# GpSimd's arithmetic moved to VectorE in every layer, and the side tasks of the first feed forward layer left unsplit

## The chip, the cores and the metric

The kernel runs on one core of a Trainium2 chip. A core has TensorE (PE) for matmuls, VectorE (DVE), ScalarE (ACT) and GpSimd (POOL) for work on elements, and queues that start DMA transfers; almost all of these are started from SyncE (SP). The time is the device time of one execution in microseconds (us), the median of 3 runs, lower is better.

## The reference

The program is a net of two blocks over 256 tokens of width 1024, all in fp32:

```python
def first_block(x, ...):
    for l in range(2):
        h = rms_norm(x, norm_mix[l])
        x = x + hybrid_mixer(h, w_in[l], ...)
        h2 = rms_norm(x, norm_mlp[l])
        x = x + jnp.square(jax.nn.relu(h2 @ w_up[l])) @ w_down[l]     # 1024 -> 4096 -> 1024
...
def second_block(x, mem, ...):
    mem_n = rms_norm_2(mem, mem_norm_g)
    for i in range(2):
        u = rms_norm_2(h, mix_norm_g[i])
        # i = 0: hyena (short convolution, then two long ones by FFT with filters from a small sine net)
        # i = 1: attention with 12 query heads and 4 key heads
        main = ...
        cross = memory_cross_attn(cq, mem_n, w_mem_kv[i])
        h = h + jnp.concatenate([main, cross], axis=-1) @ w_out[i]
        h = h + expert_choice_ffn(rms_norm_2(h, ffn_norm_g[i]), ...)  # 16 experts, 32 tokens each
    return rms_norm_2(h, final_norm_g)
```

The hyena filters and the keys and values of the memory `mem` depend on no token: they can be made at any time before the hyena layer.

## The kernel before

The stages run one after the other: mixer 0, feed forward 0, mixer 1, feed forward 1 (block 1), then hyena, experts 0, attention, experts 1 (block 2). The residual `X` stays in SBUF, and weights stream in once, through a ring of buffers (`ring.one`, `load`, line 187).

**Split products.** A dense product in fp32 is done as three matmuls in the faster format fp32r (`mm3`, lines 303 to 306): high part by high part, and two cross terms. For the weights `split` (lines 284 to 293) makes the parts: ScalarE writes `hi` (line 291), and the subtraction for `lo` (line 292) goes to the next engine of a cycle, which each stage sets: `LO0` for both feed forward layers (`mlp`, line 964), `LO1` for the hyena layer (line 1310), `LO2` for attention (line 1438), `LO3` for the attention's output product (line 1562). The mixers have VectorE alone (line 822).

```python
    lo_engines = [cycle((V,))]
    LO0 = (G, V)
...
        S.activation(hi, src, AF.Copy)
        next(lo_engines[0]).tensor_tensor(lo, src, hi.bitcast(F32), op=ALU.subtract)
```

**Order of the work.** `Pipe` (lines 89 to 135) takes units, each with a `prep` (the splits) and a `run` (the matmuls), and prepares two units ahead of the one that runs. After each unit it steps the side tasks, generators that go on to their next `yield`. A scheduler then orders each engine's instructions when the program is built.

**Feed forward** (`mlp`, lines 963 to 1025): in eight rounds of 512 hidden columns, `up` gives ReLU (line 1007), square `r` (line 1008), its high part `hh` (line 1009) and low part `hlo` (line 1012); `down` adds into four accumulators `acc`.

**Side tasks of feed forward 0.** `filters_task` makes the hyena filters: two sine layers (`sin_layer`, lines 1046 to 1061), then four rounds (two filters, two halves of 384 channels). A round makes `hd` by split matmuls (lines 1122 and 1123), adds its absolute values into `sab` (line 1130, GpSimd), forms sum and difference `hx` and splits those into `hs` (line 1137, GpSimd), sums `sab` over the tokens (`psn`, line 1142) into `nrm`, and transforms by `mm3` with `fFh`, `fFl` into `kx`. `memory_task` (line 1161 on) normalises `mem` (`Norm`, transposes at line 344, `xl` at line 348) and makes keys and values of two layers from `nm.xh` and `nm.xl` with split weights.

**Hyena** (`hyena_layer`): four `chain` tasks carry the long convolutions beside the projections; GpSimd has `ya` (line 1375), four of the sixteen `yl` (line 1380) and three `al` (line 1401). **Attention**: GpSimd makes the rotated copies `rot` (line 1466). **Routing** of the experts (`id`, `sel`, `rp`, `affb`, lines 1573 to 1654) and the product with the last gain use GpSimd too.

Of the kernel before, what the change touches and what calls it, by code (L numbers as in the profile page):

```python
# [12 lines left out]
F32 = mybir.dt.float32  # L13
# [5 lines left out]
ALU = mybir.AluOpType  # L19
# [180 lines left out]
def build(ctx, tc, I, C, out, upto="all", dbg=None):  # L200
# [78 lines left out]
    LO0 = (G, V)  # L279
    LO1 = (G, V)  # L280
    LO2 = (V, G, V)
    LO3 = (G, V)
# [43 lines left out]
    class Norm:  # L326
# [706 lines left out]
    def stream(units, pool):  # L1033

        ahead = deque()
        for u in units + [None, None]:
            if u:
                hl.append(pool)
                u.prep()
                hl.pop()  # L1040
                ahead.append(u)
            if len(ahead) == 3 or not u:
                ahead.popleft().run()
            yield

# [17 lines left out]
    def filters_task(ring, kd):  # L1063

        with tc.tile_pool(name="fl", bufs=1) as fp:
# [26 lines left out]
            hst = fp.tile([128, T], F32R, name="fhst")  # L1092
# [3 lines left out]
            S.activation(hst, h2, AF.Copy)  # L1096
            V.tensor_tensor(hst[64:], h2[64:], hst[64:].bitcast(F32), op=ALU.subtract)
# [5 lines left out]
            for o in range(2):  # L1103
                for n in range(2):
                    c = slice(384 * n, 384 * n + 384)
                    w3 = fp.tile([128, 2, 384], F32, name="fw3")
                    for d in range(2):
                        nc.sync.dma_start(w3[64 * d:64 * d + 64], I["hy_filt_w3_2"][0].rearrange("k (o d c) -> k o d c", o=2, d=2)[:, o, :, c])
                    w3h = fp.tile([128, 2, 384], F32R, name="fw3h")
                    w3l = fp.tile([64, 2, 384], F32R, name="fw3l")  # L1110
                    S.activation(w3h, w3, AF.Copy)
                    G.tensor_tensor(w3l, w3[:64], w3h[:64].bitcast(F32), op=ALU.subtract)
                    hs = {op: [fp.tile([128, 2, 384], F32R, tag=f"h{op}{i}", name="hs") for i in range(2)] for op in (ALU.add, ALU.subtract)}
                    sab = fp.tile([128, 384], F32, tag="sab", name="sab")
                    yield
                    for t in range(2):
                        hd = []
                        for d in range(2):
                            h = fp.tile([128, 384], F32, tag=f"hd{d}", name="hd")
                            ps = A("psf", [128, 384])  # L1120
                            sl = slice(t * 128, (t + 1) * 128)
                            PE.matmul(ps, hst[:, sl], w3h[:, d], start=True, stop=False)
                            PE.matmul(ps, hst[:64, sl], w3l[:, d], start=False, stop=True)
                            V.tensor_tensor(h, ps, dec[:, t, c], op=ALU.mult)
                            if t == 0 and d == 0:
                                S.activation(sab, h, AF.Abs)
                            else:
                                ab = fp.tile([128, 384], F32, tag="ab", name="ab")
                                S.activation(ab, h, AF.Abs)
                                G.tensor_tensor(sab, sab, ab, op=ALU.add)  # L1130
                            hd.append(h)
                        yield
                        for op, dst in hs.items():
                            x = fp.tile([128, 384], F32, tag="hx", name="hx")
# [10 lines left out]
                    for part, op in ((0, ALU.add), (1, ALU.subtract)):  # L1145
# [3 lines left out]
                        for t in range(2):  # L1149
                            mm3(pp[t], Fh[:, t, part], Fl[:, t, part], hs[op][0][:, t], hs[op][1][:, t], True, True)  # L1150
# [10 lines left out]
    def memory_task(ring, mp, sp, m, kvd):  # L1161

        nm = Norm(m, gain("mem_norm_g_2"), mp, A)
        yield from nm.task(lambda n: True)
        for l in range(2):
# [3 lines left out]

            def put_k(j, ps):  # L1170
                V.tensor_tensor(kv[:, 0], ps, nm.R[:, None, :].to_broadcast([128, 2, T]), op=ALU.mult)

            def put_v(ps):
                for t in range(2):
                    evac(kv[:, 1, t], ps[t][:, :256], t, nm.r[:, t:t + 1])
# [133 lines left out]
    def hyena_layer(hy, ring, nm, c2, kd, kvd, state):  # L1309
# [29 lines left out]
        def chain(o, n):  # L1339
# [22 lines left out]
            for f in range(2):  # L1362
# [24 lines left out]
            for cb in range(3):  # L1387
# [9 lines left out]
                if o:  # L1397
# [3 lines left out]
                    (V if n else G).tensor_tensor(al[:, b], sz, ah[:, b].bitcast(F32), op=ALU.subtract)  # L1401
# [35 lines left out]
    def attention_layer(late, pool, ring, nm, c2, kvd, state, wqk):  # L1437
# [17 lines left out]
        def rotate(i):  # L1455
# [7 lines left out]
            for t in range(2):  # L1463
                for j, a, nh in ((1, 768, 4), (0, 512, 4)) if i else ((0, 0, 8),):
                    for g in range(2):
                        G.tensor_tensor(hx(rot[:, t, a:a + 64 * nh])[:, :, :, g], hx(qk[:, t, a:a + 64 * nh])[:, :, :, 1 - g],
# [367 lines left out]
    def mlp0_tasks(ring):  # L1834
        yield from filters_task(ring, kd)
        with tc.tile_pool(name="memp", bufs=1) as mp, tc.tile_pool(name="mems", bufs=3) as sp:
# [4 lines left out]
            yield from memory_task(ring, mp, sp, m, kvd)  # L1841
# [183 lines left out]
```

## Time and profile before

| what | value |
|---|---|
| median of 3 runs | 1873.15 us (1870.21 to 1873.5) |
| the profiled execution | 1872.64 us, span 1870.8 us |
| mean granted clock of TensorE | 0.959 of full speed |
| TensorE busy | 1628.8 us, 87% of the span |
| VectorE busy | 985.2 us, 53% |
| ScalarE busy | 676.6 us, 36% |
| GpSimd busy | 315.1 us, 17% |

The page comes from one execution. A share is the busy time over the whole span, so it mixes stages with different limits. "Idle before" is the time that an engine waited ahead of an instruction, with what ended the wait.

### The profile page before, as it was taken

How to read it: one execution, taken by the hardware profiler on the slowest of the kernel's cores; microseconds unless marked ns; L12 is line 12 of the kernel's file. 1: busy time of each engine (PE TensorE's matmuls, PEld its weight loads, DVE VectorE, ACT ScalarE, POOL GpSimd, SP SyncE). 2: the span in 40 equal slices, each digit the busy share in tenths (PEclk: the TensorE clock that was granted, in tenths of full speed). 3: DMA queues.
4: the chain of work that ended last, by engine and by line, in shares of the span. 5: the costliest groups of instructions: out<-in, count | busy, mean ns of one | idle time of the engine just before them, and what ended most of it. 6: DMA issues, size and time to landing. Idle time of an engine off the chain costs nothing. (4 is left out here: it accounts for less than half of the span.)

```text
span 1870.8 us, 27208 instructions
## 1 busy us (share of the span) xinstructions
PE 1628.8 (87%) x11139; PEld 1195.2 (64%) x11139; DVE 985.2 (53%) x1740; ACT 676.6 (36%) x1118; POOL 315.1 (17%) x216
## 2 busy tenths in 40 slices
PE   8999999998999999999989988666667989776765
PEld 7998977788999989999878844212224655221221
DVE  6998686775579977645578752000006862110102
ACT  6446454554454555544445331000003652000001
POOL 1000026654300000444333300000002210000001
PEclk9999999999999999999999988898989999899888
DMA  7543564454644436755244689999998759999997
GB/s 257 160 137 125 172 201 160 164 203 161 209 142 147 130 124 203 278 185 196 99 153 157 254 353 425 425 426 424 426 405 315 272 203 401 425 425 425 425 421 274
DMA packets 136516, 490.41 MB, mean 262 GB/s; under 512 B 11153, under 2 KB 32068, under 8 KB 115912
## 3 DMA queue, kind: packets, MB, share of 16 engines
q1 hardware_dynamic: 135919, 488.11, 69.2%
q8 instruction: 87, 1.43, 0.3%
q10 hardware_dynamic: 472, 0.57, 0.1%
q14 instruction: 38, 0.30, 0.0%
HBM read 483.41 MB, written 5.24 MB: 261 GB/s over the span
## 5 line engine op out<-in xcount | busy, mean ns | idle before, releaser
L291 ACT ACTIVATE hi<-w 128x1024 fp32r<-128x1024 f32 (+3 forms) x330 | 328.0, 997 | 323.7 <-PE psT L306 162.3
L304 PE MATMUL psT<-xh,hi 128*128 128x256 f32 x1328 | 386.8, 291 | 0.9 <-ACT hi L291 0.9
L305 PE MATMUL psT<-xh,lo 128*128 128x256 f32 x1328 | 378.6, 285 | 4.6 <-POOL lo L292 2.7
L306 PE MATMUL psT<-xl,hi 128*128 128x256 f32 x1328 | 378.7, 285 | 0.0
L292 DVE TENSOR_TENSOR lo<-w,hi 128x1024 fp32r<-128x1024 f32 (+3 forms) x245 | 285.3, 1165 | 141.5 <-ACT hi L291 140.6
L292 POOL TENSOR_TENSOR lo<-w,hi 128x1024 fp32r<-128x1024 f32 (+1 forms) x85 | 205.0, 2413 | 590.2 <-ACT hi L291 584.6
L305 PEld LDWEIGHTS psT<-xh,lo 128*128 128x128 f32 x1328 | 256.4, 193 | 9.5 <-POOL lo L292 3.3
L304 PEld LDWEIGHTS psT<-xh,hi 128*128 128x128 f32 x1328 | 256.5, 193 | 9.2 <-issue 6.4
L306 PEld LDWEIGHTS psT<-xl,hi 128*128 128x128 f32 x1328 | 256.1, 193 | 1.4 <-issue 1.1
L1741 PE MATMUL psx<-w,late 128*32 128x256 f32 (+1 forms) x1024 | 154.4, 549 | 75.8 <-DMA w<-in_exp_w_gate 39.5
L1741 PEld LDWEIGHTS psx<-w,late 128*32 128x32 f32 x1024 | 47.1, 116 | 180.5 <-issue 74.9
L1741 PE MATMUL psx<-w,xg 128*32 128x256 f32 (+1 forms) x1024 | 124.3, 547 | 35.2 <-DMA w<-in_exp_w_up 19.7
L1793 PE MATMUL psy<-w,late 128*32 128x512 f32 x576 | 98.8, 601 | 33.7 <-DMA w<-in_exp_w_down 29.8
L1777 ACT ACTIVATE yy<-psy,rslot 128x512 fp32r<-128x512 f32 (+1 forms) x17 | 11.3, 662 | 320.6 <-PE psy L1793 253.7
L1741 PEld LDWEIGHTS psx<-w,xg 128*32 128x32 f32 x1024 | 40.5, 117 | 115.7 <-issue 60.6
L306 PE MATMUL acc<-lo,hh 128*128 128x512 f32 x256 | 100.8, 394 | 3.0 <-POOL lo L292 3.0
L305 PE MATMUL acc<-hi,hlo 128*128 128x512 f32 x256 | 100.8, 394 | 0.0
L304 PE MATMUL acc<-hi,hh 128*128 128x512 f32 x256 | 100.5, 392 | 0.0
L1778 DVE SCALAR_TENSOR_TENSOR yy<-psy,rslot,yy 128x512 fp32r<-128x512 f32 (+1 forms) x17 | 12.2, 720 | 162.0 <-ACT yy L1777 161.5
L1757 DVE TENSOR_TENSOR late<-late,psx 128x512 f32<-128x512 f32 (+1 forms) x16 | 8.1, 550 | 166.3 <-PE psx L1741 166.3
L1793 PEld LDWEIGHTS psy<-w,late 128*32 128x32 f32 x576 | 27.1, 110 | 101.1 <-DMA w<-in_exp_w_down 49.8
L1756 DVE SCALAR_TENSOR_TENSOR late<-psx,rslot,late 128x512 f32<-128x512 f32 (+1 forms) x16 | 9.1, 613 | 152.3 <-ACT late L1755 152.3
(495 smaller groups left out, 2850.1 us busy)
## 6 DMA issues: line engine op xcount, KB each, us to landing
w<-in_exp_w_gate SPq DMA_DIRECT2D x64, 1536.0 KB, 27.6
w<-in_exp_w_up SPq DMA_DIRECT2D x64, 1536.0 KB, 29.5
w<-in_exp_w_down SPq DMA_DIRECT2D x48, 1536.0 KB, 26.9
w<-in_w_in SPq DMA_DIRECT2D x39, 1024.0 KB, 5.2
w<-in_w_up SPq DMA_DIRECT2D x32, 1024.0 KB, 5.6
w<-in_w_down SPq DMA_DIRECT2D x32, 1024.0 KB, 7.1
w<-in_exp_w_down SPq DMA_DIRECT2D x18, 1024.0 KB, 14.2
w<-in_w_out SPq DMA_DIRECT2D x10, 1024.0 KB, 5.6
```

The lines of the kernel that those rows point to most:

```text
L291: S.activation(hi, src, AF.Copy)
L292: next(lo_engines[0]).tensor_tensor(lo, src, hi.bitcast(F32), op=ALU.subtract)
L304: PE.matmul(ps, lh, rh, start=start, stop=False)
L305: PE.matmul(ps, ll, rh, start=False, stop=False)
L306: PE.matmul(ps, lh, rl, start=False, stop=stop)
L1741: mm = PE.matmul(pg[nm][n][32 * e:32 * e + 32, :c1 - c0], xg[gr // 2][:, k, 128 * (gr % 2) + 32 * e:128 * (gr % 2) + 32 * e + 32], wt[e][: ...
L1756: V.scalar_tensor_tensor(sg[:, :n], pg["gate"][i][:, :n], r2, sg[:, :n], op0=ALU.mult, op1=ALU.mult)
L1757: V.tensor_tensor(hid[:, c], sg[:, :n], pg["up"][i][:, :n], op=ALU.mult)
L1777: S.activation(yh, py, AF.Copy, scale=rs[:, 2, gr:gr + 1])
L1778: V.scalar_tensor_tensor(yl, py, rs[:, 2, gr:gr + 1], yh.bitcast(F32), op0=ALU.mult, op1=ALU.subtract)
L1793: PE.matmul(py[n][32 * e:32 * e + 32], hT[:, k, 32 * e:32 * e + 32], wt[e][:, k - k0, 512 * n:512 * n + 512], start=k == 0, stop=k == 5, t ...
```

## The change

VectorE takes the subtractions for `lo` everywhere, and the single operations of the hyena layer, of attention and of the filters that GpSimd had. In the side tasks of feed forward 0 the splits are gone: filters and memory products run as plain fp32 matmuls, the two halves of `hd` in the upper and the lower 64 rows of the array (`tile_position`). The filter's third weight is loaded as [128, 384], half as many bytes, and in two buffers. The ring load of `const_fwd` in the filters becomes one direct load of the quarter that is used. The pool `mems` and the function `stream` go, and the side tasks have 64 steps in place of 70. GpSimd keeps its memsets, the routing and the last product: 45 rows of the order in place of 122; VectorE has 1528 in place of 1445, ScalarE 720 in place of 757, TensorE 7320 in place of 7563, SP 175 in place of 176.

```diff
-    LO0 = (G, V)
-    LO1 = (G, V)
-    LO2 = (V, G, V)
-    LO3 = (G, V)
+    LO0 = (V,)
+    LO1 = LO2 = LO3 = (V,)
...
         def __init__(self, src, g, pool=None, psum=None, split=True):
-            if split:
+            self.x = None
+            if split is None:
+                self.x = pool.tile([128, 8, T], F32, name="xT")
+            elif split:
...
+                    if self.x is not None:
+                        S.activation(self.x[:, k], ps[:, j], AF.Copy, scale=self.g[:, k:k + 1])
+                        continue
...
     def filters_task(ring, kd):
-            raw = ring.one(C["fwd"]).rearrange("p t (s f) -> p t s f", s=2)[:, :, :, :128]
-            Fh = fp.tile([128, 2, 2, 128], F32R, name="fFh")
-            Fl = fp.tile([128, 2, 2, 128], F32R, name="fFl")
-            S.activation(Fh, raw, AF.Copy)
-            V.tensor_tensor(Fl, raw, Fh.bitcast(F32), op=ALU.subtract)
+            F = fp.tile([128, 2, 2, 128], F32, name="fF")
+            nc.sync.dma_start(F, C["fwd"].rearrange("p t (s f) -> p t s f", s=2)[:, :, :, :128])
...
-            S.activation(hst, h2, AF.Copy)
-            V.tensor_tensor(hst[64:], h2[64:], hst[64:].bitcast(F32), op=ALU.subtract)
...
-                    w3 = fp.tile([128, 2, 384], F32, name="fw3")
+                    w3 = fp.tile([128, 384], F32, name="fw3", bufs=2)
...
-                    S.activation(w3h, w3, AF.Copy)
-                    G.tensor_tensor(w3l, w3[:64], w3h[:64].bitcast(F32), op=ALU.subtract)
...
+                        pd = [A("psf", [128, 384]) for _ in range(2)]
+                        for d in range(2):
+                            r = slice(64 * d, 64 * d + 64)
+                            PE.matmul(pd[d], h2[r, sl], w3[r], start=True, stop=True, tile_position=(64 * d, 0))
...
-                            PE.matmul(ps, hst[:, sl], w3h[:, d], start=True, stop=False)
-                            PE.matmul(ps, hst[:64, sl], w3l[:, d], start=False, stop=True)
-                            V.tensor_tensor(h, ps, dec[:, t, c], op=ALU.mult)
+                            V.tensor_tensor(h, pd[d], dec[:, t, c], op=ALU.mult)
...
-                                G.tensor_tensor(sab, sab, ab, op=ALU.add)
+                                V.tensor_tensor(sab, sab, ab, op=ALU.add)
...
-                            V.tensor_tensor(x, hd[0], hd[1], op=op)
-                            S.activation(dst[0][:, t], x, AF.Copy)
-                            G.tensor_tensor(dst[1][:, t], x, dst[0][:, t].bitcast(F32), op=ALU.subtract)
+                            V.tensor_tensor(dst[:, t], hd[0], hd[1], op=op)
...
-                            mm3(pp[t], Fh[:, t, part], Fl[:, t, part], hs[op][0][:, t], hs[op][1][:, t], True, True)
+                            PE.matmul(pp[t], F[:, t, part], hs[op][:, t], start=True, stop=True)
...
+    def memory_task(ring, mp, m, kvd):
+        nm = Norm(m, gain("mem_norm_g_2"), mp, A, None)
...
+            ps = A("psT", [128, 2, T])
+            for i in range(2):
+                for q in range(2):
+                    for k in range(4):
+                        PE.matmul(ps[:, q], w[i][:, k, 128 * q:128 * q + 128], nm.x[:, 4 * i + k],
+                                  start=i == 0 and q == 0 and k == 0, stop=i == 1 and q == 1 and k == 3)
+                yield
+            V.tensor_tensor(kv[:, 0], ps, nm.R[:, None, :].to_broadcast([128, 2, T]), op=ALU.mult)
...
+                        PE.matmul(ps[t][:, :256], nm.x[:, k, t * 128:(t + 1) * 128], w[k // 4][:, k % 4, 256:],
+                                  start=k == 0, stop=k == 7)
...
-            yield from stream(dense_T(ring, None, nm.xh, nm.xl, put_k, tiles=[x[:, :, :256] for x in w]), sp)
-            yield from stream(dense_M(ring, None, nm.xh, nm.xl, put_v, tiles=[x[:, :, 256:] for x in w]), sp)
...
-                G.tensor_tensor(a[0], a[0], a[1], op=ALU.subtract)
+                V.tensor_tensor(a[0], a[0], a[1], op=ALU.subtract)
...
-                    (G if part and not o else V).tensor_tensor(yl[:, b], a[2 * part], yh[:, b].bitcast(F32), op=ALU.subtract)
+                    V.tensor_tensor(yl[:, b], a[2 * part], yh[:, b].bitcast(F32), op=ALU.subtract)
...
-                    (V if n else G).tensor_tensor(al[:, b], sz, ah[:, b].bitcast(F32), op=ALU.subtract)
+                    V.tensor_tensor(al[:, b], sz, ah[:, b].bitcast(F32), op=ALU.subtract)
...
-                        G.tensor_tensor(hx(rot[:, t, a:a + 64 * nh])[:, :, :, g], ...
+                        V.tensor_tensor(hx(rot[:, t, a:a + 64 * nh])[:, :, :, g], ...
```

VectorE's order in a filter round of feed forward 0, before:

```order
L1124 TENSOR_TENSOR hd<-psf,dec 128x384 x2
L292 TENSOR_TENSOR lo<-w,hi 128x1024
L1135 TENSOR_TENSOR hx<-hd 128x384 x2
L1008 TENSOR_TENSOR r<-r 128x512
L1012 TENSOR_TENSOR hlo<-r,hh 128x512
L1124 TENSOR_TENSOR hd<-psf,dec 128x384 x2
```

and the same place now (lines above 290 have moved by some numbers: 292 is 290, 1008 is 1012, 1012 is 1016, 1124 is 1106):

```order
L1106 TENSOR_TENSOR hd<-psf,dec 128x384 x2
L1116 TENSOR_TENSOR hs<-hd 128x384 x2
L1112 TENSOR_TENSOR sab<-sab,ab 128x384
L1012 TENSOR_TENSOR r<-r 128x512
L290 TENSOR_TENSOR lo<-w,hi 128x1024
L1016 TENSOR_TENSOR hlo<-r,hh 128x512
L1106 TENSOR_TENSOR hd<-psf,dec 128x384
L290 TENSOR_TENSOR lo<-w,hi 128x1024
L1112 TENSOR_TENSOR sab<-sab,ab 128x384
L1106 TENSOR_TENSOR hd<-psf,dec 128x384
```

Every `lo` is now here, `sab` has come in between `hd` and `hd`, and the sums go straight to `hs`.

GpSimd's order at the routing of experts 0 (`one`, `id` and `sel` are tables of the routing, `rp` and `affb` low parts of its operands), before:

```order
L1573 MEMSET one_11371 16x1
L1575 TENSOR_SCALAR id_11373<-ident 16x16
L1577 TENSOR_TENSOR sel<-ident 128x16
L1579 TENSOR_TENSOR sel<-sel,ident 128x16 x2
L292 TENSOR_TENSOR hl<-w,hl 128x512
L1654 TENSOR_TENSOR rp<-X,rp 128x256 x2
L1620 CAST affb<-aff 128x16
```

and now:

```order
L1560 MEMSET one_11055 16x1
L1562 ISA
L1562 TENSOR_SCALAR id_11057<-ident 16x16
L1564 TENSOR_TENSOR sel<-ident 128x16
L1641 TENSOR_TENSOR rp<-X,rp 128x256
L1566 TENSOR_TENSOR sel<-sel,ident 128x16
L1641 TENSOR_TENSOR rp<-X,rp 128x256
L1566 TENSOR_TENSOR sel<-sel,ident 128x16
L1607 CAST affb<-aff 128x16
```

`ISA` is the load of GpSimd's instruction library, which stands ahead of its first arithmetic. Before, that was the first `lo` of feed forward 0.

## Rows read from the trace of the kernel before

**Rows 1.** Span by stage: stretch, length, busy PE PEld DVE ACT POOL, clock, DMA share, GB/s.

```profile
245.00:506.00 261.00, 243.36 (x1517) 213.26 (x1516) 170.50 (x206) 128.27 (x186) 134.58 (x70) 0.99 0.55 186
...
748.00:928.00 180.00, 179.99 (x1160) 164.49 (x1159) 96.35 (x92) 87.65 (x104) 77.57 (x33) 1.00 0.55 190
928.00:1100.00 172.00, 150.91 (x987) 133.20 (x986) 133.49 (x249) 76.37 (x150) 54.96 (x41) 0.97 0.59 216
1100.00:1400.00 300.00, 219.40 (x1509) 80.99 (x1508) 36.53 (x67) 22.33 (x38) 0.00 (x0) 0.92 0.99 414
1400.00:1530.00 130.00, 116.56 (x584) 75.77 (x576) 90.38 (x230) 69.86 (x160) 33.66 (x34) 0.94 0.73 269
```

**Rows 2.** VectorE groups, 748 to 925 us: count | busy us, mean ns | idle.

```profile
L292 DVE TENSOR_TENSOR lo<-w,hi 128x1024 fp32r<-128x1024 f32 x31 | 37.8, 1219 | 50.3 <-ACT hi L291 50.3
```

**Rows 3.** The tile `hlo`: count, duration in ns (min/median/max), first and last start.

```profile
L1012 DVE TENSOR_TENSOR hlo<-r,hh x32: 681/2470/2489, 272.1 to 914.2; 128x512 fp32r<-128x512 f32 x32
```

**Rows 4.** Timeline, second feed forward layer: start, duration, engine, line, [idle before <- what ended it].

```profile
801.58 2.40 POOL L292 TENSOR_TENSOR lo<-w,hi 128x1024 fp32r<-128x1024 f32 x1 [4.11 <-ACT hi L291]
...
802.05 2.47 DVE L1012 TENSOR_TENSOR hlo<-r,hh 128x512 fp32r<-128x512 f32 x1 [0.77 <-ACT hh L1009]
```

**Rows 5.** Waits of PE, first feed forward layer (245 to 506 us): total us, times, longest.

```profile
PE pst L344 <- DVE xl L348: 4.8, 1, 4.8
PE psf L304 <- DVE nrm L1143: 3.6, 4, 0.9
PE acc L306 <- POOL lo L292: 3.0, 4, 0.8
PE psf L1122 <- DVE fhst L1097: 2.1, 1, 2.1
PE psn L1142 <- POOL sab L1130: 2.1, 3, 0.9
PE psf L1094 <- ACT fh L1061: 2.0, 1, 2.0
```

**Rows 6.** The stretch after the wait for `fh`, same columns as in rows 1.

```profile
266.00:268.00 2.00, 2.00 (x10) 1.95 (x10) 1.81 (x2) 0.07 (x1) 1.85 (x1) 0.50 0.91 286
```

**Rows 7.** Timeline of PE: mixer 0, a filter round of the first feed forward layer, attention.

```profile
142.30 0.59 PE L745 MATMUL psl<-kbd,dqT 128*128 128x256 f32 x2
142.73 0.27 PE L746 MATMUL psl<-m,negI 128*128 128x256 bf16 x1
...
283.22 0.28 PE L304 MATMUL psT<-xh,hi 128*128 128x256 f32 x1
...
283.57 0.34 PE L1122 MATMUL psf<-fw3h,fhst 128*128 128x384 f32 x1
...
284.94 0.38 PE L304 MATMUL psT<-xh,hi 128*128 128x256 f32 x1
...
1486.51 1.09 PE L1215 MATMUL psv<-pT,avv 128*64 128x256 f32 x8
```

**Rows 8.** Waits of PE in the hyena stage (928 to 1100 us).

```profile
PE psr L371 <- DVE nrb L366: 3.3, 1, 3.3
PE pst L1352 <- DVE ux L1404: 3.0, 3, 1.5
...
PE psy L304 <- ACT yh L1379: 2.1, 2, 1.4
```

**Rows 9.** Timeline of VectorE, start of the hyena stage.

```profile
936.54 2.19 DVE L360 TENSOR_TENSOR ms<-ss 128x2 f32<-128x2 f32 x1
```

**Rows 10.** Timeline of POOL and PE: first arithmetic of POOL, routing of experts 0.

```profile
249.73 2.39 POOL L292 TENSOR_TENSOR lo<-w,hi 128x1024 fp32r<-128x1024 f32 x1 [11.65 <-ACT hi L291]
...
1077.14 0.09 POOL L1573 MEMSET one<- 16x1 f32 x1 [4.01 <-DVE sz L1399]
...
1087.91 0.85 POOL L1654 TENSOR_TENSOR rp<-X,rp 128x256 fp32r<-128x256 f32 x1 [0.80 <-ACT rp L1651]
...
1088.71 0.62 PE L1605 MATMUL lg<-sel,xg 128*128 128x16 f32 x4 [0.75 <-ACT xg L1601]
```

More of the change, by code (lines that the diff above doesn't have):

```diff
@@ L1031, in wait @@
             yield
[L1033 to L1044, printed above, removed]
     def sin_layer(ps, b, fr, out, pool):
@@ L1091, in filters_task @@
             h2 = fp.tile([128, T], F32, name="fh2")
-            hst = fp.tile([128, T], F32R, name="fhst")
             ps = A("psf", [128, T])
@@ L1105, in filters_task @@
                     c = slice(384 * n, 384 * n + 384)
-                    w3 = fp.tile([128, 2, 384], F32, name="fw3")
+                    w3 = fp.tile([128, 384], F32, name="fw3", bufs=2)
                     for d in range(2):
-                        nc.sync.dma_start(w3[64 * d:64 * d + 64], I["hy_filt_w3_2"][0].rearrange("k (o d c) -> k o d c", o=2, d=2)[:, o, :, c])
-                    w3h = fp.tile([128, 2, 384], F32R, name="fw3h")
-                    w3l = fp.tile([64, 2, 384], F32R, name="fw3l")
-                    S.activation(w3h, w3, AF.Copy)
-                    G.tensor_tensor(w3l, w3[:64], w3h[:64].bitcast(F32), op=ALU.subtract)
-                    hs = {op: [fp.tile([128, 2, 384], F32R, tag=f"h{op}{i}", name="hs") for i in range(2)] for op in (ALU.add, ALU.subtract)}
+                        nc.sync.dma_start(w3[64 * d:64 * d + 64], I["hy_filt_w3_2"][0].rearrange("k (o d c) -> k o d c", o=2, d=2)[:, o, d, c])
+                    hs = {op: fp.tile([128, 2, 384], F32, tag=f"h{op}", name="hs") for op in (ALU.add, ALU.subtract)}
                     sab = fp.tile([128, 384], F32, tag="sab", name="sab")
@@ L1117, in filters_task @@
                         hd = []
+                        sl = slice(t * 128, (t + 1) * 128)
+                        pd = [A("psf", [128, 384]) for _ in range(2)]
+                        for d in range(2):
+                            r = slice(64 * d, 64 * d + 64)
+                            PE.matmul(pd[d], h2[r, sl], w3[r], start=True, stop=True, tile_position=(64 * d, 0))
                         for d in range(2):
                             h = fp.tile([128, 384], F32, tag=f"hd{d}", name="hd")
-                            ps = A("psf", [128, 384])
-                            sl = slice(t * 128, (t + 1) * 128)
-                            PE.matmul(ps, hst[:, sl], w3h[:, d], start=True, stop=False)
-                            PE.matmul(ps, hst[:64, sl], w3l[:, d], start=False, stop=True)
-                            V.tensor_tensor(h, ps, dec[:, t, c], op=ALU.mult)
+                            V.tensor_tensor(h, pd[d], dec[:, t, c], op=ALU.mult)
                             if t == 0 and d == 0:
@@ L1159, in filters_task @@
             V.reciprocal(rn, nrm)
-    def memory_task(ring, mp, sp, m, kvd):
-        nm = Norm(m, gain("mem_norm_g_2"), mp, A)
+    def memory_task(ring, mp, m, kvd):
+        nm = Norm(m, gain("mem_norm_g_2"), mp, A, None)
         yield from nm.task(lambda n: True)
@@ L1168, in memory_task @@
             yield
-            def put_k(j, ps):
-                V.tensor_tensor(kv[:, 0], ps, nm.R[:, None, :].to_broadcast([128, 2, T]), op=ALU.mult)
-            def put_v(ps):
-                for t in range(2):
-                    evac(kv[:, 1, t], ps[t][:, :256], t, nm.r[:, t:t + 1])
-            yield from stream(dense_T(ring, None, nm.xh, nm.xl, put_k, tiles=[x[:, :, :256] for x in w]), sp)
-            yield from stream(dense_M(ring, None, nm.xh, nm.xl, put_v, tiles=[x[:, :, 256:] for x in w]), sp)
+            yield
[5 more added lines that the diff above has]
+                                  start=i == 0 and q == 0 and k == 0, stop=i == 1 and q == 1 and k == 3)
+                yield
+            V.tensor_tensor(kv[:, 0], ps, nm.R[:, None, :].to_broadcast([128, 2, T]), op=ALU.mult)
+            ps = [A("psM") for _ in range(2)]
+            for k0 in range(0, 8, 2):
+                for t in range(2):
+                    for k in (k0, k0 + 1):
+                        PE.matmul(ps[t][:, :256], nm.x[:, k, t * 128:(t + 1) * 128], w[k // 4][:, k % 4, 256:],
+                                  start=k == 0, stop=k == 7)
+                yield
+            for t in range(2):
+                evac(kv[:, 1, t], ps[t][:, :256], t, nm.r[:, t:t + 1])
             nc.sync.dma_start(kvd[l], kv)
@@ L1465, in rotate @@
                     for g in range(2):
-                        G.tensor_tensor(hx(rot[:, t, a:a + 64 * nh])[:, :, :, g], hx(qk[:, t, a:a + 64 * nh])[:, :, :, 1 - g],
+                        V.tensor_tensor(hx(rot[:, t, a:a + 64 * nh])[:, :, :, g], hx(qk[:, t, a:a + 64 * nh])[:, :, :, 1 - g],
                                         xhf(tg[:, j, t, 1])[:, None, :, g].to_broadcast([128, nh, 2, 16]), op=ALU.mult)
@@ L1835, in mlp0_tasks @@
         yield from filters_task(ring, kd)
-        with tc.tile_pool(name="memp", bufs=1) as mp, tc.tile_pool(name="mems", bufs=3) as sp:
+        with tc.tile_pool(name="memp", bufs=1) as mp:
             m = mp.tile([128, 2, D], F32, name="mem")
@@ L1840, in mlp0_tasks @@
                 yield
-            yield from memory_task(ring, mp, sp, m, kvd)
+            yield from memory_task(ring, mp, m, kvd)
     c2s = ctx
```

1 line of the change is left out of this document (removed).

## The prediction, as it stood before the changed kernel ran

> **What bounds the kernel now.** I began with the head of the page: a span of 1870.8 us, in an execution of 1872.64, so 1.8 us lie outside the span. That execution is 0.5 us under the median of the runs shown (1873.15): a difference against this execution is one against the median too. Next I cut the span at the stages [rows 1]. TensorE is busy for 243.36 of the 261 us of the first feed forward layer, for 179.99 of 180 in the second, for 150.91 of 172 in the hyena stage: a feed forward layer lasts as long as its matmuls plus their gaps. In the experts' stage the DMA share is 0.99 at 414 GB/s. Nothing on VectorE or GpSimd shortens that one, and a gain made before it moves it forward whole, since its loads begin when the stage before frees their slots.
>
> GpSimd is busy for 134.58 us of the first feed forward layer and 77.57 of the second. What that costs shows less in GpSimd's rows than in VectorE's. In the second layer `lo` takes 1219 ns on VectorE [rows 2], while `hlo`, half as wide, has a median of 2470 over its 32, with a minimum of 681 [rows 3]. Two rows of the timeline say why [rows 4]: at 801.58 GpSimd begins a `lo` of 2.40 us, and at 802.05 VectorE begins `hlo`, which takes 2.47. With 0.68 it would have ended 1.2 us before GpSimd did; it ended 0.5 us after. So a VectorE operation on two SBUF operands stands still while GpSimd computes: a GpSimd `lo` buys 1.22 us of VectorE work for 2.40 us in which VectorE may stand.
>
> Only waits of TensorE turn that into time. In the first feed forward layer there are 14 in six groups, 17.6 us together [rows 5]; the rest is matmuls.
>
> **The change, part by part.**
>
> (a) First feed forward layer: every `lo` goes to VectorE, and the side tasks (hyena filters, memory keys and values) lose their splits. Five of the six groups of waits end with something that the change removes or frees. `xl` of the memory norm (4.8) and `fhst` (2.1) are no longer made; `lo` (3.0) and `sab` (2.1) no longer come from GpSimd; `fh` (2.0) ends a chain of sine steps whose VectorE part GpSimd held up. The four waits for `nrm` (3.6) stay, for the sum, its evacuation and the transform follow each other as before. That is 17.6 - 3.6 = 14.0 us. After two of the waits the granted clock fell to 0.50, the lower level of 1.2 GHz [rows 6]; ten matmuls began in those 2.00 us, 0.20 us apart, where it is otherwise three in 0.35 (283.22 to 283.57) [rows 7], 0.117 apart. Some twelve at 0.20 - 0.117 make 1.0 us, twice 2.0. Waits gone: 16.0 us.
>
> Against it stands what unsplit matmuls cost TensorE. A plain fp32 matmul of 256 columns takes 0.43 us (142.30 to 142.73), a split product 3 x 0.117 = 0.35 [rows 7]. Memory keys and values: 64 products, 192 x 0.117 = 22.5 us before, 64 x 0.43 = 27.5 after, +5.0. Filter transform `kx`, 384 columns, both prices scaled by 1.5: 48 x 0.175 = 8.4 before, 16 x 0.645 = 10.3 after, +1.9. The filter itself, `hd`: a pair took 1.37 us (283.57 to 284.94), eight are 11.0. After, it is 16 matmuls over 64 rows each; end to end that is 16 x 0.645 = 10.3. But a pair sits in two halves of the array, and where two halves of its columns were used, four 256-column matmuls (eight records) took 1.09 us in place of 4 x 0.43 = 1.72 [rows 7]. At that ratio it is 6.5. No row has halves by rows; the nearest overlaps, so I take -4.5, and -0.7 is the other end. Net +2.4, at most +6.2.
>
> The sum of (a) is -16.0 + 2.4 = -13.6, rounded **-14**. The ends: -17.5, if the `nrm` waits go too, and -2, if half of the waits come back at another place and `hd` does not overlap.
>
> The Trainium skill ("FP8 and Floating Point Precision", section "TensorE Precision Notes") has true fp32 take four passes of the array. At 4 x 0.117 = 0.47 us, an estimate from that page and a row, memory and `kx` would cost 3.3 us more, and the sum would end near 1853. The row of 0.43 decides.
>
> Can VectorE carry it? GpSimd's 134.58 us are worth, at 1.22 to 2.40, at most 68 us of VectorE, and the part that only made splits goes. With its 170.50 [rows 1] that is at most 239 of some 247 us, even if none of its standing still went; but `hlo` alone should give back (2.47 - 0.68) for most of its sixteen. I charge nothing. Two details: in the new order a `sab` that waits for ScalarE's absolute value stands ahead of an `hd` in VectorE's queue, a delay of one ScalarE operation in a task that is spread over the whole layer. And SP's queue loses the ring load of `fwd`; the smaller load of `fF` is issued in the first step of the task, several steps ahead of its use. Their cover is the other matmuls, of which TensorE's queue always has a unit; without it each round would show one wait of the size of `sab`'s, 0.7 us, eight rounds 5.6, inside the upper end.
>
> (b) Second feed forward layer: TensorE is busy for 179.99 of 180, and VectorE's 96.35, with half of GpSimd's 77.57 added, would be 136 of 180 at most. **0**.
>
> (c) Into the hyena stage. TensorE waits 3.3 us for `nrb` [rows 8], at the end of a VectorE chain in which operations on two columns take 2.19 us (936.54) while GpSimd is at work [rows 9]. Three of these follow each other; freed, the chain is 6.2 us shorter, but three `lo` of 1.22 (3.7) join its queue. **-2.5**, from 0 to -5.6.
>
> (d) Rest of the hyena stage. The waits with a VectorE chain behind them are three groups, for `ux` (3.0), `uv` and `yh` (2.1), 7.7 us in all [rows 8]. VectorE gets 54.96 x 0.51 = 28 us at most on top of its 133.49, and loses the standing still that GpSimd's 54.96 us made in it: about a draw in load, with shorter chains. I take half the waits, **-4**. If all go it is -9, with the clock that a gap costs; if a third of the 28 us comes where TensorE is waiting, +9.
>
> (e) Attention: TensorE idles for 13.4 of 130 us, and VectorE takes 33.66 x 0.51 = 17 us on top of 90.38 [rows 1]. Fewer of its operations meet GpSimd here, so less comes back: **-3**, a quarter of the idle time, from -5 to +6, a third of the 17.
>
> (f) GpSimd's first arithmetic instruction has a library load ahead of it (`ISA` in the order). Before, it fell into 11.65 us of idle time before the first `lo`; now it stands in the first routing, between `one`, which began at 1077.14, and `sel`, which a matmul at 1088.71 reads [rows 10]. At its greatest, 11.65, it would end about when that matmul now starts, and `sel` would be late by the short operations behind the load, an estimated 3.5 us; at its least, nothing. For the load I take nothing, since 11.65 is an idle time and only bounds it. I take **+0.5**, which comes from the order alone: the last step of `sel` now stands behind both `rp`, whose second ended at 1087.91 + 0.85 = 1088.76 [rows 10], and so ends some 0.4 after the old start of the matmul.
>
> Sum: -14 - 2.5 - 4 - 3 + 0.5 = -23; 1872.64 - 23 = **1850**.
>
> **The rivals.**
>
> A, only the first feed forward layer pays (0.22): what VectorE takes on in the hyena stage and in attention eats what its freed operations return, the draw of (d). 1872.64 - 14 = 1859.
>
> B, more than forecast (0.15): in (c), (d) and (e) the waits go nearly whole, towards the lower ends -5.6, -9 and -5, in place of -9.5 together: some 10 us less, 1840.
>
> C, VectorE becomes the bound (0.08). If `hlo` and its like are long for another reason than GpSimd, they stay long and the moved work is pure addition: 239 of 247 us in the first feed forward layer, 133 + 28 = 161 of 172 in hyena, 107 of 130 in attention. Then TensorE waits for `lo` again and again; a third of the 28 and of the 17 us, 15, comes out as time, and the gain of (a) is not made: 1872.64 + 15 + 2.4 = 1890. It decides where `hlo` stays above 2 us with GpSimd idle. Against it: the minimum of 681 ns [rows 3], and [rows 4]. The Trainium skill ("Perfetto Trace Analysis", section "Optimizing Scalar/DVE Operations") speaks for C: with VectorE saturated, it says, work may be moved to GpSimd; it adds that the port they share may spoil this, and the second half is what [rows 4] show.
>
> D, no change (0.05): the waits of (a) come back behind ScalarE's `hi`, which each `lo` needs, and the plain matmuls take what is left: 1873. GpSimd keeps some arithmetic in any case, in the routing and at the end.
>
> **How the numbers follow.** Forecast 0.50, A 0.22, B 0.15, C 0.08, D 0.05. About 0.2% (3.7 us) is what a measurement of this kernel can tell from no change. Faster: 0.50 + 0.22 + 0.15 = 0.87; same 0.05; slower 0.08. The range holds the forecast, A and B with a few us around the outer two, 1837 to 1865, and leaves out C and D.
>
> **What would show it.** Right: `hlo` near 0.68 us throughout; the waits of the first feed forward layer down to those for `nrm`, and that layer about 247 us long; operations on two columns back to a few tenths of a us; the second layer unchanged. Wrong: waits for VectorE's `lo` or `kx` in the first layer, memory matmuls of more than 0.43 us each, a hyena stage longer than 172 us less 6.5, or a routing that waits for `sel`.

## The result, and the profile after

The changed kernel takes **1830.33 us** (4 runs, 1826.36 to 1833.79) against 1873.33: a ratio of 0.9774, 95% interval 0.9751 to 0.9796. In a later series it took 1831.42, 0.9778 (0.9763 to 0.9792). It is faster, as forecast, but by 41 to 43 us where 23 were forecast, and 1830 lies below the range of 1837 to 1865.

The stages, each from the first start of an instruction to the first start of the next one in the list (VectorE's first addition to `X` from a feed forward layer, the routing's `lg`, attention's `cqT`), in us, all from profiled executions:

| stage | before | after | difference | forecast |
|---|---|---|---|---|
| mixer 0 | 241.6 | 242.4 | +0.8 | 0 |
| first feed forward layer | 260.2 | 239.0 | -21.2 | -14 |
| mixer 1, second feed forward layer | 425.9 | 425.6 | -0.3 | 0 |
| hyena, up to the routing's `lg` | 161.0 | 143.8 | -17.2 | -6 |
| experts 0 into attention | 357.3 | 357.2 | -0.1 | 0 |
| rest of attention, up to `lg` | 83.1 | 79.2 | -3.9 | -3 |
| experts 1 and the end | 341.7 | 342.0 | +0.3 | 0 |

The span by stage, columns as in [rows 1] (the third row is hyena up to `lg`):

```profile
245.00:485.50 240.50, 240.48 (x1440) 207.53 (x1439) 149.85 (x234) 110.81 (x154) 0.00 (x0) 1.00 0.57 194
727.50:907.00 179.50, 179.49 (x1157) 164.11 (x1157) 105.39 (x129) 87.64 (x104) 0.96 (x1) 1.00 0.56 192
907.00:1050.80 143.80, 140.00 (x961) 126.15 (x959) 124.24 (x254) 76.40 (x146) 3.55 (x7) 1.00 0.65 233
1361.50:1488.00 126.50, 115.36 (x584) 75.06 (x576) 92.64 (x255) 69.71 (x160) 5.29 (x9) 0.94 0.74 275
```

TensorE is busy for 240.48 of 240.50 us in the first feed forward layer: the trace lists no wait of TensorE there, where [rows 5] had 14. VectorE, with 67 `lo` of 128x1024 where it had 34, is busy for 149.85 us, less than the 170.50 of [rows 1]. In the hyena stage the kernel before, cut the same way, reads (compare the third row above):

```profile
927.80:1088.70 160.90, 144.19 (x959) 129.49 (x957) 125.33 (x220) 75.18 (x146) 54.70 (x40) 0.98 0.57 205
```

TensorE idled for 160.90 - 144.19 = 16.7 us and now for 3.8; its busy time fell by another 4.2, with the granted clock up from 0.98 to 1.00. VectorE's busy time is the same (125.33, 124.24), with 34 operations more.

Three of TensorE's waits there, against [rows 8] (total us, times, longest), and the one wait of the kernel before that bears GpSimd's name; then the first step of the short convolution on VectorE, before and after (columns as in [rows 2]); and the tile `hlo`, against [rows 3]:

```profile
PE psy L302 <- ACT yh L1366: 0.5, 1, 0.5
...
PE psy L303 <- DVE yl L1367: 0.4, 1, 0.4
PE psr L375 <- DVE nrb L370: 0.3, 1, 0.3
```

```profile
PE psT L305 <- POOL lo L292: 1.3, 1, 1.3
```

```profile
L1333 DVE SCALAR_TENSOR_TENSOR ux<-tmp,sw,ux 128x255 f32<-128x255 f32 x12 | 12.3, 1052 | 2.7 <-ACT ux L1332 2.7
```

```profile
L1320 DVE SCALAR_TENSOR_TENSOR ux<-tmp,sw,ux 128x255 f32<-128x255 f32 x12 | 5.3, 481 | 0.7 <-ACT ux L1319 0.7
```

```profile
L1016 DVE TENSOR_TENSOR hlo<-r,hh x32: 683/684/689, 268.4 to 894.1; 128x512 fp32r<-128x512 f32 x32
```

No wait for `ux` or `uv` is left, `nrb` is down from 3.3 to 0.3, the longest wait of the stage is one of 0.6, and `hlo` takes 684 ns in the median where it took 2470.

### The profile page after: what moved, and what is told of

The parts are those of the page before. It is cut to its first block, busy times and chain, and to the rows that moved or that the text cites. A ratio compares the mean times of both kernels' runs of the same rounds, so it can differ in the third digit from the quotient of the medians.

```text
span 1829.2 us, 26865 instructions
## 1 busy us (share of the span) xinstructions
PE 1616.7 (88%) x11059; PEld 1182.8 (65%) x11059; DVE 973.0 (53%) x1858; ACT 658.5 (36%) x1084; POOL 24.1 (1%) x56
## 4 chain that ended last, share of the span: by engine, by line
PE 62%; DMA 29%; DVE 5%; ACT 2%; issue 1%; SPq 1%; ACTq 0%; DVEq 0%
DMA w<-in_exp_w_up 10%; DMA w<-in_exp_w_gate 10%; DMA w<-in_exp_w_down 9%; PE psT L302 9%; PE psT L303 9%; PE psT L304 9%; PE acc L302 3%; PE acc L303 3%; PE acc L304 3%; PE psM L302 3%; PE psM L303 3%; PE psM L304 3%; PE psx L1728 2%; PE psl L1184 1%; PE psy L1794 1%
## 5 line engine op out<-in xcount | busy, mean ns | idle before, releaser
L290 DVE TENSOR_TENSOR lo<-w,hi 128x1024 fp32r<-128x1024 f32 (+3 forms) x318 | 368.1, 1159 | 170.2 <-ACT hi L289 166.3
L289 ACT ACTIVATE hi<-w 128x1024 fp32r<-128x1024 f32 (+3 forms) x318 | 320.0, 1007 | 372.1 <-PE psT L304 166.2
L302 PE MATMUL psT<-xh,hi 128*128 128x256 f32 x1296 | 376.3, 291 | 0.9 <-ACT hi L289 0.9
L303 PE MATMUL psT<-xh,lo 128*128 128x256 f32 x1296 | 367.1, 283 | 1.2 <-DVE lo L290 1.2
L304 PE MATMUL psT<-xl,hi 128*128 128x256 f32 x1296 | 366.4, 283 | 0.0
L302 PEld LDWEIGHTS psT<-xh,hi 128*128 128x128 f32 x1296 | 247.8, 191 | 11.4 <-issue 8.7
L303 PEld LDWEIGHTS psT<-xh,lo 128*128 128x128 f32 x1296 | 247.9, 191 | 6.2 <-DVE lo L290 1.9
L304 PEld LDWEIGHTS psT<-xl,hi 128*128 128x128 f32 x1296 | 247.7, 191 | 0.8 <-issue 0.7
L302 PE MATMUL acc<-hi,hh 128*128 128x512 f32 x256 | 104.6, 408 | 0.0
L1765 DVE SCALAR_TENSOR_TENSOR yy<-psy,rslot,yy 128x512 fp32r<-128x512 f32 (+1 forms) x17 | 12.2, 720 | 161.4 <-ACT yy L1764 161.0
L1742 ACT ACTIVATE late<-psx,rslot 128x512 f32<-128x512 f32 (+1 forms) x16 | 8.4, 577 | 198.8 <-PE psx L1728 172.0
```

The costliest lines, as they stand in the source:

```text
L302: PE.matmul(ps, lh, rh, start=start, stop=False)
L303: PE.matmul(ps, ll, rh, start=False, stop=False)
L304: PE.matmul(ps, lh, rl, start=False, stop=stop)
L1765: V.scalar_tensor_tensor(yl, py, rs[:, 2, gr:gr + 1], yh.bitcast(F32), op0=ALU.mult, op1=ALU.subtract)
```

## The experiments

Three theories. **1**: VectorE's operations stand still while GpSimd computes, so VectorE runs late and TensorE waits. **2**: GpSimd's own results came late, since it takes 2.4 us where VectorE takes 1.2. **3**: in the first feed forward layer the gain is that of the unsplit side tasks.

### Low parts alone

On the kernel before:

```diff
-    LO0 = (G, V)
-    LO1 = (G, V)
-    LO2 = (V, G, V)
-    LO3 = (G, V)
+    LO0 = (V,)
+    LO1 = LO2 = LO3 = (V,)
```

> The kernel before with one edit: every low part of a weight goes to VectorE (LO0 to LO3 are V alone); the side tasks stay split, and GpSimd keeps its work in the filters, the hyena chain and attention. Theory 1 (VectorE stands still while GpSimd computes, and TensorE waits for the late VectorE): most of the gain outside the first feed forward layer comes from here, since the lows are 26 + 11 of GpSimd's 55 us in the hyena stage: hyena -12 to -17 us, attention -2 to -4. In the first feed forward layer GpSimd keeps 43 of 135 us (filter operations), so about half of that layer's 21 us: -8 to -14. Total 1840 to 1850. Theory 2 (TensorE waited because GpSimd's own results came late, 2.4 us in place of 1.2): only the waits named after GpSimd's lows go, 3.0 + 1.3 + 1.4 us, total 1863 to 1869. Theory 3 (the gain of the first layer is the unsplit side tasks): that layer gains 3 us here.

Measured: 1829.7 us, ratio 0.9786 (0.9773 to 0.98). These four lines carry the whole gain, more than any of the theories gave them. The first feed forward layer takes 239.1 us, hyena 146.8, the rest of attention 79.5. (Hyena is 3 us longer than in the changed kernel, but the stage of experts 0 is 3.9 shorter in this profile, 353.3, and that stage varies from 353 to 360 between the runs; so the total does not show the 3.) In the first layer GpSimd still works for 46 us, and TensorE's waits are down to three:

```profile
PE pst L342 <- DVE xl L346: 1.2, 1, 1.2
PE psf L1120 <- DVE fhst L1095: 0.6, 1, 0.6
PE acc L304 <- DVE lo L290: 0.2, 1, 0.2
```

### Side tasks alone

On the changed kernel:

```diff
-    LO0 = (V,)
-    LO1 = LO2 = LO3 = (V,)
+    LO0 = (G, V)
+    LO1 = (G, V)
+    LO2 = (V, G, V)
+    LO3 = (G, V)
...
-                V.tensor_tensor(a[0], a[0], a[1], op=ALU.subtract)
+                G.tensor_tensor(a[0], a[0], a[1], op=ALU.subtract)
```

(`yl`, `al` and `rot` go back to GpSimd in the same way.)

> The changed kernel with GpSimd put back everywhere but in the side tasks (LO0 to LO3 as before, GpSimd in the hyena chain and in attention): the unsplit side tasks alone. Theory 1: GpSimd keeps 92 of its 135 us in the first feed forward layer, hlo stays near 2.4 us there; the waits for xl (4.8) and fhst (2.1) go, because the operations are gone, the others stay or return under other names; that layer -8 to -14, the rest of the program 0. Total 1859 to 1865. Theory 3: that layer gains its whole 21 us here, total 1850 to 1853.

Measured: 1851.99 us, ratio 0.9895 (0.9881 to 0.9908). The first feed forward layer takes 240.2 us, as theory 3 had it. But `hlo` there still takes 2278 ns in the mean:

```profile
L1018 DVE TENSOR_TENSOR hlo<-r,hh 128x512 fp32r<-128x512 f32 x16 | 36.5, 2278 | 11.0 <-ACT hh L1015 11.0
```

and TensorE's waits are 0.8 us. So in this layer **each half of the change takes nearly the whole 21 us by itself**, and the two together take no more. Neither GpSimd's low parts nor the split side tasks make TensorE wait much alone; without waits the layer is as long as its matmuls. The reading that fits is that only both at once put VectorE and GpSimd behind by more than the two units that are prepared ahead. It is not shown: either half also takes work off GpSimd, whose busy time in the layer falls from 134.58 us to 46 with the low parts moved and to 78 here, and no run parts that from the rest.

Hyena took 157.8 here, 3.2 us less than before, with the same code. The wait for `nrb` (3.3) is gone from its list; the others stayed, within 0.4. The difference arises there: the first product `psz` starts 40.6 us after the stage's start in the kernel before and 37.1 here, and what follows keeps that distance to 0.3. In the chain that ends in `nrb`, an operation on two columns met a GpSimd `lo` before (first two rows), and here (last two) the `lo` came 1.5 us behind it:

```profile
947.02 2.35 POOL L292 TENSOR_TENSOR lo<-w,hi 128x1024 fp32r<-128x1024 f32 x1 [5.94 <-ACT hi L291]
947.07 2.33 DVE L321 TENSOR_TENSOR rt<-rh,nr 128x2 f32<-128x2 f32 x1
```

```profile
927.79 0.15 DVE L321 TENSOR_TENSOR rt<-rh,nr 128x2 f32<-128x2 f32 x1
929.26 2.40 POOL L292 TENSOR_TENSOR lo<-w,hi 128x1024 fp32r<-128x1024 f32 x1 [7.45 <-ACT hi L291]
```

VectorE's chain so ends 2.2 us earlier after the stage's start. The rest of the 3.3 is not the chain's: TensorE also came to `nrb` later, with a granted clock of 0.67 in the 6 us ahead of it, against 1.00 before. A part of what GpSimd costs is thus a matter of which operation it happens to meet.

### The memory task split again

On the changed kernel:

```diff
-        nm = Norm(m, gain("mem_norm_g_2"), mp, A, None)
+        nm = Norm(m, gain("mem_norm_g_2"), mp, A)
...
+            yield from stream(dense_T(ring, None, nm.xh, nm.xl, put_k, tiles=[x[:, :, :256] for x in w]), sp)
+            yield from stream(dense_M(ring, None, nm.xh, nm.xl, put_v, tiles=[x[:, :, 256:] for x in w]), sp)
```

> The changed kernel with the memory task split again (three fp32r matmuls per product, low parts on VectorE); the filters stay unsplit. The unsplit memory matmuls cost TensorE 5 us more than the split ones (64 x 0.43 against 192 x 0.117). If VectorE has room now (150 of 236 us busy), the layer becomes 5 us shorter: 1825. If the memory norm's xl or the eight half-width lows come late again on their own account and not on GpSimd's, waits of TensorE for xl (4.8 before) return: 1830 to 1835.

Measured: **1824.94 us**, ratio 0.9749 (0.9735 to 0.9762), the fastest kernel of the study, 5.4 and 6.5 us below the changed one's two medians, which are from other series; its interval lies just below that of the changed kernel in the second one (0.9763 to 0.9792) and overlaps that in the first (0.9751 to 0.9796). The stage shows it more safely: the first feed forward layer takes 235.8 us, 3.2 less, with one wait of 1.3 for `xl`; the rest of the difference lies in experts 0, whose length goes from 353 to 360 us between the profiles here. Since TensorE bounds that layer once the waits are gone, the unsplit memory matmuls are a cost. In the changed kernel eight of them (sixteen records) read

```profile
415.21 3.62 PE L1153 MATMUL psT<-xT,w 128*128 128x256 f32 x16
418.47 0.58 PE L302 MATMUL acc<-hi,hh 128*128 128x512 f32 x1
418.90 0.40 PE L303 MATMUL acc<-hi,hlo 128*128 128x512 f32 x1
```

The next matmul begins 3.26 us later, and the one after it 0.43 after that instead of the usual 0.23: 3.46 us for eight, 0.43 each, as [rows 7] had it. The Trainium skill ("FP8 and Floating Point Precision", section "TensorE Precision Notes") has such a product take four passes of the array; at 0.117 each that is an estimate of 0.47. These rows show 3.7 times the 0.117 of a single one.

### Idle GpSimd work in the first feed forward layer

On the changed kernel, in `split`, in that layer alone, at every second low part:

```diff
+                G.tensor_tensor(idle["t"].rearrange("p (a b) -> p a b", a=shape[1]), src, src, op=ALU.subtract)
```

> The changed kernel with 32 idle GpSimd subtractions of 128x1024 in the first feed forward layer, into a tile that nobody reads (the result of the program is the same). Nothing waits for GpSimd's results. Theory 1: VectorE's operations on two SBUF operands stretch again (hlo back above 1.5 us in the median of that layer), VectorE runs late and TensorE's waits come back under names of VectorE and ScalarE: +5 to +15 us, 1835 to 1845. Theory 2: no change, 1829 to 1832.

Measured: 1836.07 us, ratio 0.9807 (0.9794 to 0.9821). The layer takes 246.5 us, 7.5 more; all other stages are within 1.6 us of the changed kernel's. Nobody waits for the idle operations (the dummies, below), so theory 2 falls as the whole cause. But `hlo` is long in some places only (mean 1000 ns, median of both layers 684), and the time goes at one place, the sine steps at the layer's start:

```profile
PE psf L1109 <- ACT fh L1058: 3.3, 1, 3.3
PE psf L1087 <- ACT fh L1058: 2.6, 1, 2.6
```

### Idle GpSimd work in the hyena stage

On the changed kernel, in `split`, in the hyena stage alone, at every second low part, in pieces of 256 columns:

```diff
+                    G.tensor_tensor(d if key == 2 else d.rearrange("p (a b) -> p a b", a=shape[1] // 4), s, s, op=ALU.subtract)
```

> The changed kernel with 56 idle GpSimd subtractions of 128x256 in the hyena stage (the same number of elements as the low parts that GpSimd had there before), written to padding that nobody reads. Nothing waits for them. Theory 1 (VectorE stands still while GpSimd computes): VectorE's chain runs late, L1333 stretches again to about 1 us in the mean, TensorE's waits for ux, uv and nrb return, and the stage up to the routing takes 150 to 158 us in place of 143.8: total 1836 to 1844. Theory 2 (GpSimd's own results came late): no change, 1828 to 1832.

Measured, with the changed kernel at 1831.42 in the same series: 1839.06 us, ratio 0.9819 (0.9806 to 0.9833). The stage takes 152.0 us, 8.2 more:

```profile
906.90:1058.90 152.00, 142.07 (x958) 127.54 (x957) 133.20 (x253) 76.56 (x146) 40.71 (x52) 0.99 0.60 219
```

The waits for `nrb` (3.4), `uv` (1.7) and `ux` (1.2) are back. Nobody waits for the dummies. They read the weights alone, so they ran when these arrived, not when low parts used to be made; 11 of the 56 ran before the stage began.

### Low parts of hyena and attention on GpSimd, the rest on VectorE

On the changed kernel:

```diff
-    LO1 = LO2 = LO3 = (V,)
+    LO1 = (G, V)
+    LO2 = (V, G, V)
+    LO3 = (G, V)
```

> The changed kernel with the low parts of hyena and attention back on GpSimd in turn (LO1 to LO3 as before), the single operations of both stages on VectorE. It parts the 17 us of the hyena stage into low parts and chain operations. From the run with the low parts alone moved (hyena stage 146.8, attention 79.5) I expect the low parts to carry all but 3 us: hyena stage 155 to 159, attention 81 to 83, total 1844 to 1850. If chain operations and low parts each relieve VectorE enough by themselves, as the two halves of the change did in the first feed forward layer: hyena 145 to 149, total 1832 to 1836.

Measured: 1854.5 us, ratio 0.9908 (0.9895 to 0.9922). Hyena takes 163.4 us, 2.4 **more** than before and more than the 155 to 159 that I expected; the rest of attention 80.0. Moving the single operations (`ya`, `yl`, `al`, `rot`) alone does nothing good: VectorE then has more to do and still meets GpSimd's low parts. With the low parts gone as well, those of the hyena chain are worth 146.8 - 143.8 = 3 us.

```profile
907.20:1070.70 163.50, 145.88 (x960) 131.22 (x959) 131.80 (x236) 75.23 (x146) 39.27 (x25) 0.96 0.57 203
```

### The rest of GpSimd's arithmetic

On the kernel with the memory task split again:

```diff
-            lo(k, G)
+            lo(k)
...
-        G.tensor_copy(affb, aff[:, 0])
+        V.tensor_copy(affb, aff[:, 0])
```

(and `id64`, `sel` and the product with the last gain.)

> The changed kernel with the memory task split again and the rest of GpSimd's arithmetic (routing tables, two low parts in each routing, the product with the last gain) on VectorE. By theory 1 the routing's VectorE chain loses its stretched operations, 0.5 to 1 us for each routing and 0.5 at the end, against 1 us of added work: 1823 to 1826, no measurable gain over the split memory task alone (1824.9).

Measured: 1826.43 us, ratio 0.9759 (0.9746 to 0.9773): no gain over 1824.94, as expected. Hyena is within 0.1 us of the changed kernel's, the rest of attention 0.4 longer, and the first feed forward layer takes 234.5, so the gain of the split memory task stands in a second run. The changed kernel itself ran in this series for comparison:

> The changed kernel once more, beside the other runs of this call: 1828 to 1832. Against it the split memory task (1824.9 in the first call) is to be judged.

Measured: 1831.42 us, with its stages at the same 239.0 and 143.8.

### Idle GpSimd work at the old places

On the changed kernel, in `split`, in the first feed forward layer and the hyena stage, at every second low part:

```diff
+                for i in range(0, shape[1], m):
+                    s, h = src[:, i:i + m], hi[:, i:i + m].bitcast(F32)
+                    d = t[:, :m] if flat else t[:, :m * shape[2]].rearrange("p (a b) -> p a b", a=m)
+                    G.tensor_tensor(d, s, h, op=ALU.subtract)
```

> The changed kernel with idle GpSimd subtractions that start when the low parts of the kernel before started: beside every second low part on VectorE, in the first feed forward layer and the hyena stage, GpSimd does the same subtraction into a tile that nobody reads (in pieces of 256 in the hyena stage). It parts standing still from late results: the dummies have GpSimd's old timing and load of low parts, but no one waits for their results. If standing still is the whole of it, the hyena stage goes from 143.8 to 158 or more (163.4 with the low parts themselves on GpSimd), and the first feed forward layer, whose side tasks stay unsplit, keeps 239 to 241, as with the low parts themselves there (240.2): total 1843 to 1850. If late results of GpSimd are the larger part, the hyena stage stays at 148 to 153, as with the unpaced dummies (152.0): total 1834 to 1840.

Measured: 1863.08 us (6 runs, 1857.36 to 1864.19), ratio 0.9942 (0.9925 to 0.9959), 32 to 33 us above the changed kernel's medians in the other series, from operations whose results nobody reads. VectorE, ScalarE and TensorE have the changed kernel's order in both stages, but for a few places. The profile is of the fastest of the six runs, so what the stages show, +20 and +9 us, is less than the median's 32. Hyena takes 163.7 us, where the low parts themselves on GpSimd gave 163.4:

```profile
916.00:1079.70 163.70, 146.44 (x960) 130.36 (x958) 144.93 (x253) 76.84 (x146) 61.66 (x63) 0.97 0.55 197
```

```profile
PE psr L387 <- DVE nrb L382: 4.4, 1, 4.4
PE pst L1351 <- DVE ux L1403: 2.3, 1, 2.3
PE pst L1351 <- DVE uv L1333: 2.1, 3, 1.1
```

The dummies also hold `hi` and the weights a little longer; in the hyena stage ScalarE waited for them once, for 2.1 us, and SyncE's queue twice, for 6.2, but no engine waited for a weight. So in the hyena stage **VectorE's standing still is enough for a loss of this size**, with no late result of GpSimd in it. That it agrees with the run with the low parts themselves to 0.3 us is in part luck: GpSimd is busy for 61.66 us here and for 39.27 with the low parts themselves, and VectorE has 17 operations more. When GpSimd works seems to matter: at the old places it cost 20 us, at places set by the weights' arrival 8, though with 40.71 us of GpSimd's time in the stage. In the first feed forward layer the stage went to 248.0, 9 more, above the 241 that I expected, and `hlo` is at 2468 again. A reason would be that VectorE has its own low parts beside the dummies here; no run tests it, and ScalarE waited for the dummies there for 4.2 us.

## Why the prediction was wrong

**The mechanism was right, the sizes were not.** The three terms that take back waits in the first feed forward layer and in hyena, (a), (c) and (d), were too small; the others held.

- (b) 0, measured 0. (e) -3, measured -3.9. (f) +0.5, nothing to see: after the change `lg` waits 0.6 us for `xg` in the first routing, 0.8 for a GpSimd `rp` in the second, 0.7 to 0.8 before. The library load that (f) bounded by 11.65 us left no gap in the trace: `id`, the first arithmetic behind it, begins 0.06 us after `one` ends:

```profile
1041.27 0.09 POOL L1560 MEMSET one<- 16x1 f32 x1 [145.47 <-DVE sz L1386]
1041.42 0.25 POOL L1562 TENSOR_SCALAR id<-ident 16x16 f32<-16x16 f32 x1
```

- (a) -14, measured -21.2. Three parts of the term failed. "The four waits for `nrm` (3.6) stay, for the sum, its evacuation and the transform follow each other as before": they went. In the kernel before, the evacuation was not held up by the sum but by VectorE's queue. The rows around the first such wait:

```profile
300.24 0.34 PE L306 MATMUL psf<-hs,fFh 128*128 128x384 f32 x1
301.50 0.41 PE L304 MATMUL psf<-hs,fFh 128*128 128x384 f32 x1 [0.93 <-DVE nrm L1143]
```

```profile
300.06 1.23 DVE L292 TENSOR_TENSOR lo<-w,hi 128x1024 fp32r<-128x1024 f32 x1
301.20 0.15 DVE L1143 TENSOR_SCALAR nrm<-psn 128x3 f32<-128x3 f32 x1
```

  `nrm` came right behind a `lo`. After the change VectorE is ahead and waits for the sum itself:

```profile
288.17 0.16 DVE L1122 TENSOR_SCALAR nrm<-psn 128x3 f32<-128x3 f32 x1 [1.27 <-PE psn L1121]
```

- The second part is how a wait is counted. The row above says 0.93, but the two matmuls begin 1.26 us apart where 0.17 is usual: 1.09 lost. Matmuls overlap, and the wait counts from the modelled end of the first. Over all 14 waits the distances between starts give 19.9 us where the list of waits gave 17.6; without `nrm`, 15.6 in place of 14.0. The third is the clock after two of them: 3.0 us by the same count in place of 2.0. What is left of the 21.2 is +1.7, where the unsplit matmuls were to cost +2.4: -19.9 - 3.0 + 1.7 = -21.2. Of these the guess for `hd` held: a pair in two halves of 64 rows takes 0.85 us (278.05 to 278.90), eight 6.8, where 6.5 were taken:

```profile
278.05 0.92 PE L1103 MATMUL psf<-fw,fh 64*128 64x384 f32 x4
278.90 0.38 PE L302 MATMUL psT<-xh,hi 128*128 128x256 f32 x1
```

- (c) and (d) with (f), -6, measured -17.2, the larger miss. The step was "about a draw in load, with shorter chains. I take half the waits". The draw was right to 1.1 us (125.33 and 124.24 us busy), but it says nothing about lateness: the same busy time held 34 more operations, each done when it was due. TensorE's idle time fell from 16.7 to 3.8, that is by three quarters, and the slower clock that the waits brought with them went too (4.2 us of busy time). I had counted 3.3 + 7.7 of the 16.7, took 6.5 of these 11.0, and kept the clock to the far end of the range. Of the lower ends, -5.6 for (c) is more than the 3.3 of the wait itself and has no working, and -17.5 for (a) is -17.2 by its own terms.
- The rivals: A (only the first layer pays) is out, since hyena gives 17 us. B, more than forecast, had the right direction and stopped at 10 us. C is out: `hlo` is at 684 ns. D is out.
- What the change was worth by parts I had wrong too, and no stage total could show it: the -14 of (a) was put down to both halves together, while either half does nearly all of it alone, and the unsplit memory task, given the low parts on VectorE, costs 3 us of that layer.

## What to carry to other kernels

Where VectorE's operations on SBUF operands are several times longer than the shortest of their kind, look at what GpSimd does beside them, and price GpSimd's share by what TensorE idles in the whole stage, not by the waits that name GpSimd: of 16.7 us of idle time in the hyena stage, 1.3 had its name. When two edits relieve the same slack, try each alone: here one of them brought everything, and a part of the other (the unsplit memory task) was a loss. And count a wait of TensorE from start to start, and look at the granted clock behind it.

## What the runs showed of the hardware

That operations whose results nobody reads can cost 32 us of 1830 I had not expected; of the places tried, the worst were those beside VectorE's own low parts. GpSimd pays too: its idle `lo` took 3280 ns in the mean in the first feed forward layer when it ran beside VectorE's, where the real `lo` of the run with the side tasks alone took 2436 and the dummies at the weights' arrival 2321:

```profile
L302 POOL TENSOR_TENSOR idle<-w,hi 128x1024 f32<-128x1024 f32 x31 | 101.7, 3280 | 136.8 <-ACT hi L291 122.5 <-issue 13.9
```

That fits the Trainium skill ("SBUF — State Buffer", section "SBUF: two separate sides"): a GpSimd operation and a VectorE operation with two SBUF inputs hold a shared pair of ports for their whole length, and the later one waits. The rows agree, since each side's operations grow by no more than the other's length (2.47 - 0.68 for `hlo` in [rows 4], and in the mean 3.28 - 2.32 here). One idle `lo` took 6.50 us, more than a single VectorE operation can account for; no run tells why.

Which VectorE operations stand still shows in the kernel before, around a GpSimd `lo`. The two `kx`, with one operand in PSUM, take their usual 0.55 us beside it, and the `lo` on two SBUF operands behind them takes 2.24 in place of 1.22:

```profile
301.05 2.49 POOL L292 TENSOR_TENSOR lo<-w,hi 128x1024 fp32r<-128x1024 f32 x1 [1.58 <-ACT hi L291]
```

```profile
301.38 0.55 DVE L1152 TENSOR_TENSOR kx<-ke,psf 128x384 f32<-128x384 f32 x1
301.85 0.55 DVE L1156 TENSOR_TENSOR kx<-ke,psf 128x384 f32<-128x384 f32 x1
302.39 2.24 DVE L292 TENSOR_TENSOR lo<-w,hi 128x1024 fp32r<-128x1024 f32 x1
```

Two operands are not needed for it: the operation below reads one tensor in SBUF and took 2.33 us while GpSimd computed from 936.12 to 941.08; in the changed kernel it never takes more than 0.17:

```profile
938.77 2.33 DVE L361 TENSOR_SCALAR ms<-ms 128x2 f32<-128x2 f32 x1
```
